# Low parts of weight blocks by a second rounding pass and an accumulating DMA instead of a GpSimd subtract

## The chip, the cores and the metric

The kernel runs on one core of one Trainium2 chip. Its time is device microseconds of one execution; times of a kernel are medians of several runs. A core has the engines TensorE (PE in the profile, PEld for its weight loads), VectorE (DVE), ScalarE (ACT), GpSimd (POOL) and SyncE (SP), which work side by side, each through its own instructions in order, and wait for each other through semaphores. DMAs are issued by an engine and done by 16 DMA engines.

## The reference

One step of a two-layer decoder trunk, 1024 wide, on 1056 tokens: one new sequence of 1024 and 8 sequences of 4 tokens each that go on from stored states. Layer 0 is an RG-LRU block, layer 1 an HGRN2 block with 8 heads of 128. What matters here is layer 1's input projection and what follows it in each head:

```
xn = _rmsnorm(x, g_norm)
u = (xn @ w_in).astype(float32)            # 1056 x 1024 times 1024 x 4096
q, f, iv, gate = split(u, 4, axis=-1)
q = silu(q)
log_g = logaddexp(log(lb), log1p(-lb) + log_sigmoid(f)); k = -expm1(log_g)
o, S_T = _hgrn2_chunked(q, k, iv, log_g, S0)
y = (rmsnorm over each head of o) * silu(gate)
x = x + y @ w_out
```

All of it is float32, and the outputs are the hidden states, the recurrent states and the normalised trunk output.

## The kernel before, in words

Tokens lie on the free axis, features on the 128 partitions. A float32 product is made of three matmuls in a faster format (`F32R`): each operand is split into a high part, which is the operand rounded to that format, and a low part, which is operand minus high part. `mm3` (lines 241 to 243) adds high times high, weight high times data low, and weight low times data high. In the profile the weight parts are named `whi` and `wlo`, and a raw weight block `wraw` (some raw blocks live in a piece of the tile `R`).

Layer 1 works head by head. For heads 0 and 1 the four projections are plain products of 352 columns. For heads 2 to 7 (`HC = 2`) two projections at a time are done by `seven`: the 256 outputs and the 1024 inputs and the 1056 tokens are halved, and seven products of half-size blocks take the place of eight. So there are twelve calls of `seven`, two for each head, the first for the projections 0 and 1 (q and f), the second for 3 and 2 (gate and v). One product is 24 matmuls of 264 columns. `FQ0`, `FQ` and `GV` give the order of the seven products (digits) and where in it the bursts of the heads' attention work (letters `b`) stand on TensorE.

A call of `seven` loads four raw blocks of 128 x 512 by SP (`dma`, line 308), forms the sums and differences that the scheme needs in place by `combine` on GpSimd (line 1431), and makes the high and low part of each of the seven blocks in `split`: ScalarE copies the raw block into the rounded format (line 1423), GpSimd subtracts that from the raw block (helper `subtract`, line 321 in the profile). High and low parts have rings of `NW = 4` buffers, so a split waits until the product four places earlier is done with its buffers. The raw blocks have five places, which go from one call to the next when their last split has read them. VectorE's `plus` (line 1504) and ScalarE's copies (line 1481) take the products out of PSUM; VectorE's operations of lines 1031 (decay scaling), 1053 and 1056 (masked copies) and 1519 belong to the attention and the activations of the heads.

The order of the work on every engine is set by a planner, the class `Flow`: each operation is added with an engine, an estimated time, what it reads and writes and a priority; `run` lists the operations by their latest starts and emits them in the order of the best plan found. There are two plans, one after the other: the first ends with layer 0 and the beginning of layer 1, the second holds all calls of `seven`. TensorE's main operations keep the order in which they are added. An operation with `both` set is a VectorE one that the plan holds back while GpSimd is busy. A DMA is an operation with a size `kb`, whose landing the plan estimates from it.

Of the kernel before, what the change touches and what calls it, by code (L numbers as in the profile page):

```python
# [14 lines left out]
F32 = mybir.dt.float32  # L15
# [3 lines left out]
AF = mybir.ActivationFunctionType  # L19
ALU = mybir.AluOpType  # L20
# [189 lines left out]
def tile_trunk(ctx: ExitStack, tc: tile.TileContext, xT, prm, hc, w0, wg, wo0, w1, wo1, s_in,  # L210
               yT, h_out, c_out, sp_out, ss_out):
    nc = tc.nc
    V, S, G, T, Q = nc.vector, nc.scalar, nc.gpsimd, nc.tensor, nc.sync
# [80 lines left out]
    with ExitStack() as l0:  # L294
        pl = l0.enter_context(tc.tile_pool(name="l0", bufs=1, reuse_waits="tile"))
        fl = Flow("PE")
# [9 lines left out]

        def dma(dst, src, r=(), w=(), prio=5, kb=180, q=Q):
            fl.add("SP" if q is Q else "ACT", 0.45, lambda: q.dma_start(dst, src), r, w, prio, kb * (1.0 if r else 0.75))

        def act(n, emit, r, w, prio=5, more=0.0):  # L310
            fl.add("ACT", 0.25 + 0.0007 * n + more, emit, r, w, prio)

        def dve(n, emit, r, w, prio=5, both=False):
            fl.add("DVE", 0.13 + 0.0011 * n, emit, r, w, prio, both=both)

        def pool(n, emit, r, w, prio=5):
            fl.add("POOL", 0.1 + 0.00245 * n, emit, r, w, prio)

        def subtract(e, n, b, x, a, r, w, prio):

            emit = lambda: e.tensor_tensor(b, x, a.bitcast(F32), op=ALU.subtract)  # L321
            if e is G:
                pool(n, emit, r, w, prio)
            else:
                dve(n, emit, r, w, prio, True)
# [38 lines left out]
        def weights(src, n, prio=2, e=G, at=None, q=Q, own=()):  # L364

            own = iter(own)
            got = []
            for a in range(0, n, 512):
                m = min(512, n - a)
                raw, *rk = next(own, None) or next(raws)  # L370
                if at:
                    (hi, hk), (lo, lk) = ((o[:, a:a + m], k) for o, k in at)
                else:
                    (hi, hk), (lo, lk) = next(his), next(los)
                dma(raw[:, :m], src[:, a:a + m], (), rk, prio, m / 2, q)
                act(m, lambda hi=hi, raw=raw, m=m: S.copy(hi[:, :m], raw[:, :m]), rk, (hk,), prio)  # L376
                subtract(e, m, lo[:, :m], raw[:, :m], hi[:, :m], (*rk, hk), (lk,), prio)
                got.append((hi, lo, hk, lk))

            def get(k):  # L380
                q = slice((k % 4) * 128, (k % 4 + 1) * 128)
                hi, lo, hk, lk = got[k // 4]
                return hi[:, q], lo[:, q], (hk, lk)

            return get
# [74 lines left out]
        def conv(g, head=False):  # L460

            items = []
            for j in range(3):
# [3 lines left out]
                def evac(c, ps, pk, by=None, j=j, m=m, mine=mine):  # L467
# [25 lines left out]
                    for src, dst, sh, u in parts:  # L493
                        act(u, lambda src=src, dst=dst, sh=sh: S.activation(dst, sh(src, 3), AF.Identity, bias=pc("cb", m),  # L494
                                                                         scale=pc("cw", 36 + m)), (xk, ("P",)), (tk,), 1, 0.1)
                        for k in range(3):
                            dve(u, lambda src=src, dst=dst, sh=sh, k=k: V.scalar_tensor_tensor(  # L497
                                dst, sh(src, k), pc("cw", 12 * k + m), dst, op0=ALU.mult, op1=ALU.add), (xk, tk), (tk,), 1, True)
                    w = slice(32 * j, 32 * j + 32)
                    dma(ST[w, chunk(c)], t[w], (tk,), (("ST", j, c),), 1, 45)  # L500
                    (a, ak), (b, bk) = xpart(j, 0, c), xpart(j, 1, c)
                    act(CH, lambda: S.copy(a, t), (tk,), (ak,), 1)
# [32 lines left out]
        def lru(g):  # L535
            for i, n in ((0, 4), (4, 2)):
                raw, rk = next(raws)
                u = 128 * n
                hi = gh[:, i:i + n, :].rearrange("p a b -> p (a b)")
                lo = gl[:, i:i + n, :].rearrange("p a b -> p (a b)")  # L540
                dma(raw[:, :u], wg[g][:, 128 * i:128 * i + u], (), (rk,), 2, u / 2)
                act(u, lambda raw=raw, hi=hi, u=u: S.copy(hi, raw[:, :u]), (rk,), (("gh", i),), 2)
                pool(u, lambda raw=raw, hi=hi, lo=lo, u=u: G.tensor_tensor(lo, raw[:, :u], hi.bitcast(F32), op=ALU.subtract),
                     (rk, ("gh", i)), (("gl", i),), 2)
# [297 lines left out]
        raw = (halves[1][:8], [slots[i] for i in (1, 4, 7, 2, 5, 8)] + [halves[1][8], free[8]], free[:8])  # L842
# [82 lines left out]
    with ExitStack() as l1:  # L925
        p1 = l1.enter_context(tc.tile_pool(name="l1", bufs=1, reuse_waits="tile"))
        fl = Flow(side=0.4)
# [468 lines left out]
        def seven(h, a, b, order, at=()):  # L1396
# [24 lines left out]
            def split(p):  # L1421
                (raw, rk), (hi, hk), (lo, lk) = slot[named[p]], next(his), next(los)
                act(512, lambda: S.copy(hi, raw), (rk,), (hk,), 2)  # L1423
                subtract(G, 512, lo, raw, hi, (rk, hk), (lk,), 2)
                parts[p] = hi, lo, (hk, lk)
                if p not in (1, 2):
                    freed.append(slot[named[p]])

            def combine(o, x, y, op):
                (o, ok), (x, xk), (y, yk) = slot[o], slot[x], slot[y]  # L1430
                pool(512, lambda: G.tensor_tensor(o, x, y, op=op), (xk, yk), (ok,), 2)

            split(1)
            split(2)
            combine("s", "21", "22", ALU.add)
            combine("21", "11", "21", ALU.subtract)
            combine("11", "s", "11", ALU.subtract)
            combine("12", "12", "11", ALU.subtract)
            for p in steps[2:NW]:
                split(p)  # L1440
# [15 lines left out]
            for c in order:  # L1456
# [8 lines left out]
                hi, lo, wk = parts[p]  # L1465
# [33 lines left out]
                n = steps.index(p) + NW  # L1499
# [70 lines left out]
        for k in range(H):  # L1570
            if k < 4:
                olds = [("x", 1, k, x) for x in range(2)] + [("T", 1, i, k, x) for i in range(2) for x in range(2)]
            else:
                n, i = ((2, 0), (3, 0), (4, 0), (4, 1))[k - 4]
# [66 lines left out]
        for m in range(KD):  # L1641
            row = (xh, xl)[m // 4][4 + m % 4]
            hi, lo, hk, lk = row[:, :nl], row[:, nl:2 * nl], ("late", m, 0), ("late", m, 1)
            for k in (hk, lk):
                inherit(k, [("x", p, m % 4, x) for p in (2, 3) for x in range(2)])
            raw, rk = next(raws)
# [60 lines left out]
        for a, n in OUT:  # L1707
# [4 lines left out]
            for m in range(KD):  # L1712
# [5 lines left out]
                hi, lo, wk = late[m]  # L1718
# [97 lines left out]
```

## Time and profile before

| what | us |
|---|---|
| runs, median of 3 | 1078.3 (1077.45 to 1078.73) |
| profiled execution, its own time | 1075.47 |
| its span, first to last instruction | 1073.7 |
| PE, PEld busy in the span | 1053.0, 1024.5 |
| DVE, ACT, POOL busy in the span | 808.2, 611.1, 558.0 |
| granted TensorE clock, mean | 0.996 |

The profile is of one execution. A group's row gives line, engine, operation, output from inputs, shape and count, then busy time and the mean of one in ns, then the engine's idle time before it and what ended that. A row of the timeline gives start, length, engine, line, operation and count, and in brackets the idle time before it. Matmul rows overlap, since matmuls are pipelined: a product's pace is read from the starts. A row of a stretch gives its limits, its length, busy time and count of PE, PEld, DVE, ACT and POOL, the granted clock, the share of the DMA engines and GB/s.

### The profile page before, as it was taken

The page shows a single profiled execution, that of the slowest core. Times are in us where ns is not written, and L with a number is a line of the kernel's source. Part 1 is how long each engine was busy: PE and PEld are TensorE (multiplying, and loading weights), DVE is VectorE, ACT ScalarE, POOL GpSimd, SP SyncE. Part 2 cuts the span into 40 slices and gives each one's busy share as a digit, 9 for nine tenths or more (in the row PEclk, how much of TensorE's full clock was granted, in tenths as well). Part 3 has the DMA queues.
Part 4 walks back from the last instruction along what each step waited for, and adds up shares of the span by engine and source line. Part 5 has one row for each costly group of instructions (what it writes and reads, how often), then busy time and mean ns, then how long its engine had stood idle before and what let it go on. Part 6 is the DMA issues. An engine that isn't in the chain of part 4 may idle for free.

```text
span 1073.7 us, 25345 instructions
## 1 busy us (share of the span) xinstructions
PE 1053.0 (98%) x9972; PEld 1024.5 (95%) x9972; DVE 808.2 (75%) x1535; ACT 611.1 (57%) x1395; POOL 558.0 (52%) x546
## 2 busy tenths in 40 slices
PE   9999999999999999999999998999999999999997
PEld 9999999999999999999998997999999999989996
DVE  8999996887997787283999997767768585774446
ACT  7578656867665964243364563747474655752323
POOL 3425353353543547455574854656566665541545
PEclk9999999999999999999999999999999999999998
DMA  9101112124832775240110121212121212354204
GB/s 302 59 27 43 56 49 71 58 61 126 271 104 66 222 252 176 103 131 34 60 51 24 49 92 43 100 43 91 35 92 41 91 44 80 116 169 160 85 1 162
DMA packets 70119, 103.05 MB, mean 96 GB/s; under 512 B 9200, under 2 KB 51184, under 8 KB 70000
## 3 DMA queue, kind: packets, MB, share of 16 engines
q1 hardware_dynamic: 67696, 98.67, 28.1%
q10 hardware_dynamic: 2304, 2.77, 0.8%
q8 instruction: 78, 1.28, 0.5%
q14 instruction: 41, 0.34, 0.1%
HBM read 71.05 MB, written 25.49 MB: 90 GB/s over the span
## 4 chain that ended last, share of the span: by engine, by line
PE 82%; DVE 14%; issue 1%; DMA 1%; ACT 1%; POOL 0%; SPq 0%; POOLq 0%; ACTq 0%; DVEq 0%
PE mm L241 23%; PE mm L242 22%; PE mm L243 22%; PE hg L1049 2%; DVE R L1363 1%; DVE R L1031 1%; PE hg L1266 1%; PE hg L565 1%; DVE tmp L1363 1%; PE hg L1158 1%; DVE a L1232 1%; PE hg L1268 1%; DVE sg L1031 1%; PE hg L241 1%; PE hg L242 1%
## 5 line engine op out<-in xcount | busy, mean ns | idle before, releaser
L241 PE MATMUL mm<-xh,whi 128*128 128x352 f32 (+1 forms) x1143 | 359.3, 314 | 7.2 <-DVE sg L1504 4.5
L242 PE MATMUL mm<-xl,whi 128*128 128x352 f32 (+1 forms) x1143 | 353.2, 309 | 0.0
L243 PE MATMUL mm<-xh,wlo 128*128 128x352 f32 (+1 forms) x1143 | 353.2, 309 | 0.0
L321 POOL TENSOR_TENSOR wlo<-wraw,whi 128x512 fp32r<-128x512 f32 (+2 forms) x131 | 175.9, 1351 | 168.7 <-ACT whi L376 83.6
L241 PEld LDWEIGHTS mm<-xh,whi 128*128 128x128 f32 x1143 | 214.7, 188 | 10.5 <-DVE sg L1504 6.0
L242 PEld LDWEIGHTS mm<-xl,whi 128*128 128x128 f32 x1143 | 215.0, 188 | 1.6 <-DVE xl L321 0.2
L243 PEld LDWEIGHTS mm<-xh,wlo 128*128 128x128 f32 x1143 | 214.9, 188 | 0.0
L497 DVE SCALAR_TENSOR_TENSOR k<-xb,prm_sb,k 128x352 f32<-128x352 f32 (+2 forms) x144 | 90.1, 637 | 10.9 <-ACT k L494 6.1
L241 PE MATMUL mm<-t,whi 128*128 128x264 f32 (+1 forms) x306 | 89.5, 293 | 0.0
L242 PE MATMUL mm<-t,whi 128*128 128x264 f32 (+1 forms) x306 | 87.7, 287 | 0.0
L243 PE MATMUL mm<-t,wlo 128*128 128x264 f32 (+1 forms) x306 | 87.5, 286 | 0.0
L580 POOL TENSOR_TENSOR k<-X 128x352 f32<-128x352 f32 x36 | 44.9, 1256 | 47.8 <-DVE R L581 38.6
L321 POOL TENSOR_TENSOR wlo<-R,whi 128x512 fp32r<-128x512 f32 x33 | 49.9, 1511 | 32.8 <-ACT whi L1423 28.9
L376 ACT CAST whi<-wraw 128x512 fp32r<-128x512 f32 (+2 forms) x83 | 46.0, 574 | 28.5 <-PE mm L242 16.9
L241 PEld LDWEIGHTS mm<-t,whi 128*128 128x128 f32 x306 | 57.6, 188 | 0.7 <-ACT k L1481 0.5
L1504 DVE TENSOR_TENSOR k<-mm,k 128x264 f32<-128x264 f32 x62 | 26.5, 430 | 41.5 <-PE mm L243 41.4
L243 PEld LDWEIGHTS mm<-t,wlo 128*128 128x128 f32 x306 | 57.7, 188 | 0.0
L242 PEld LDWEIGHTS mm<-t,whi 128*128 128x128 f32 x306 | 57.6, 188 | 0.0
L1031 DVE TENSOR_TENSOR R<-R,sg 128x512 f32<-128x512 f32 (+1 forms) x48 | 50.4, 1050 | 0.1
L241 PE MATMUL mm<-yh,whi 128*128 128x352 f32 x153 | 49.9, 326 | 0.0
L243 PE MATMUL mm<-yh,wlo 128*128 128x352 f32 x153 | 49.4, 323 | 0.0
L242 PE MATMUL mm<-yl,whi 128*128 128x352 f32 x153 | 49.4, 323 | 0.0
(415 smaller groups left out, 2684.6 us busy)
## 6 DMA issues: line engine op xcount, KB each, us to landing
wraw<-in_w_dram SPq DMA_DIRECT2D x91, 256.0 KB, 2.6
wraw<-in_wo_dram SPq DMA_DIRECT2D x34, 192.0 KB, 2.5
si<-in_s_in_dram SPq DMA_DIRECT2D x8, 512.0 KB, 4.2
out_ss_out_dram<-si SPq DMA_DIRECT2D x8, 512.0 KB, 2.6
sg<-x1b SPq DMA_DIRECT2D x21, 176.0 KB, 2.8
x<-sg SPq DMA_DIRECT2D x21, 176.0 KB, 1.8
R<-in_w_dram SPq DMA_DIRECT2D x14, 256.0 KB, 2.5
R<-td SPq DMA_DIRECT2D x72, 44.0 KB, 2.0
```

The costliest lines, as they stand in the source:

```text
L241: T.matmul(out, wh, xh, start=first, stop=False, skip_group_check=chained)
L242: T.matmul(out, wh, xl, start=False, stop=False, skip_group_check=chained)
L243: T.matmul(out, wl, xh, start=False, stop=last, skip_group_check=chained)
L321: emit = lambda: e.tensor_tensor(b, x, a.bitcast(F32), op=ALU.subtract)
L376: act(m, lambda hi=hi, raw=raw, m=m: S.copy(hi[:, :m], raw[:, :m]), rk, (hk,), prio)
L497: dve(u, lambda src=src, dst=dst, sh=sh, k=k: V.scalar_tensor_tensor(dst, sh(src, k), pc("cw", 12 * k + m), dst, op0=ALU.mult, op1=ALU.add ...
L565: fl.add("PE", 0.62, lambda ps=ps, i=i, c=c: T.matmul(ps[:96, :CH], gs[:, i, :], ST[:96, chunk(c)], start=True, stop=True), (("gs",), *((" ...
L580: pool(CH, lambda x=x, a=a, b=b: G.tensor_tensor(x, a.bitcast(F32), b.bitcast(F32), op=ALU.add), (ak, bk), (xk,), 3)
L1031: dve(n // 2, lambda sv=sv, dv=dv, s=s, f=f: V.tensor_tensor(dv[:, :, s, :], sv[:, :, s, :], f, op=ALU.mult), (*sk, *gk), dk if i == o els ...
L1049: T.matmul(ps[32 * j:32 * j + 32, n * w:n * w + w], B[:, o:o + 32], q(slice(o, o + 32)), start=True, stop=True, tile_position=(0, 32 * j))
L1363: dve(n, lambda: V.tensor_tensor(o, a, b, op=op), r, (w,), prio, True)
L1504: dve(QT, lambda: V.tensor_tensor(o[0], z[0], u[0], op=ALU.add), (z[1], u[1]), (o[1],), 0)
```

## The change

`split` makes the low part in another way. ScalarE makes the high part as before. The low part's buffer is first filled by a second ScalarE pass, which writes the negated raw block rounded to the same format; then a DMA issued by GpSimd's queue adds the raw block to it where it lies, in float32. The sum is raw block minus rounded raw block, the same low part. The low part no longer reads the high part, and the raw block is read by the DMA until this has landed. GpSimd no longer subtracts in `split`. Other users of `subtract` stay as they are. For the planner the DMA is an operation of 0.93 on GpSimd with a landing.

```diff
         def dma(dst, src, r=(), w=(), prio=5, kb=180, q=Q):
             fl.add("SP" if q is Q else "ACT", 0.45, lambda: q.dma_start(dst, src), r, w, prio, kb * (1.0 if r else 0.75))
+
+        def low(n, dst, src, r, w, prio=5):
+
+            act(n, lambda: S.activation(dst, src, AF.Copy, scale=-1.0), r, w, prio)
+            fl.add("POOL", 0.93, lambda: G.dma_start(dst.bitcast(F32), src, accum_op=ALU.add), (*r, *w), w, prio, n / 2)
...
                 act(512, lambda: S.copy(hi, raw), (rk,), (hk,), 2)
-                subtract(G, 512, lo, raw, hi, (rk, hk), (lk,), 2)
+                low(512, lo, raw, (rk,), (lk,), 2)
                 parts[p] = hi, lo, (hk, lk)
```

## The prediction

> **What bounds the kernel now.** I read the page first, for the engine that is full.
>
> ```profile
> span 1073.7 us, 25345 instructions
> PE 1053.0 (98%) x9972; PEld 1024.5 (95%) x9972; DVE 808.2 (75%) x1535; ACT 611.1 (57%) x1395; POOL 558.0 (52%) x546
> ```
>
> PE (TensorE matmul) is busy 98% of the span, and the change takes nothing from it. It can only touch gaps of PE, so the next view is a table of stretches. The seven products of heads 2 to 7 run from about 589 to 926 us; what lies before 589 belongs to a first plan that the diff leaves as it is. Columns: PE, PEld, DVE, ACT, POOL busy.
>
> ```profile
> 589.00:667.00 78.00, 74.08 (x942) 70.21 (x944) 68.22 (x117) 42.57 (x123) 49.36 (x38) 1.00 0.18 64
> 725.00:783.00 58.00, 57.23 (x859) 55.15 (x846) 40.58 (x82) 34.11 (x91) 36.10 (x29) 1.00 0.19 67
> 926.00:1074.00 148.00, 138.43 (x1254) 132.67 (x1242) 81.12 (x184) 55.40 (x153) 63.83 (x68) 0.97 0.36 118
> ```
>
> The first head loses 78.00 - 74.08 = 3.9 us of PE, an ordinary head 0.77. The view of waits, cut to 589:926 and PE, says what ended these gaps:
>
> ```profile
> PE mm L241 <- DVE sg L1504: 4.3, 6, 0.8
> PE mm L241 <- DVE attns L1056: 2.7, 1, 2.7
> ```
>
> That is all: 7.0 us, and each time PE waits for DVE. No gap of this stretch is ended by the low parts themselves. So 7.0 us is the most that the change can win here, and the question is why DVE is late. The timeline of the longest gap shows it (start, length, engine):
>
> ```profile
> 642.15 4.46 DVE L1519 SCALAR_TENSOR_TENSOR sg<-sg,k 128x264 f32<-128x264 f32 x1
> 641.56 1.04 POOL L1190 TENSOR_TENSOR vb<-vst,bm 96x512 fp32r<-96x512 f32 x1 [1.58 <-DVE vst L1174]
> 642.56 1.27 POOL L321 TENSOR_TENSOR wlo<-wraw,whi 128x512 fp32r<-128x512 f32 x1
> 643.79 1.30 POOL L321 TENSOR_TENSOR wlo<-R,whi 128x512 fp32r<-128x512 f32 x1
> 645.05 1.27 POOL L1431 TENSOR_TENSOR wraw<-R,wraw 128x512 f32<-128x512 f32 x1
> 646.40 1.36 POOL L1431 TENSOR_TENSOR R<-R,wraw 128x512 f32<-128x512 f32 x1
> 650.24 0.39 PE L241 MATMUL mm<-xh,whi 128*128 128x264 f32 x1 [2.70 <-DVE attns L1056]
> ```
>
> A DVE operation with two operands in SBUF took 4.46 us while POOL went through a mask, two of the subtracts that the change removes (L321) and two block sums without a pause. The small waits have the same cause:
>
> ```profile
> 763.02 1.28 POOL L1431 TENSOR_TENSOR wraw<-R,wraw 128x512 f32<-128x512 f32 x1
> 763.16 1.69 DVE L1031 TENSOR_TENSOR sg<-sg 128x512 f32<-128x512 f32 x1
> 767.90 0.68 DVE L1031 TENSOR_TENSOR R<-R,sg 128x512 f32<-128x512 f32 x1
> 768.99 0.39 PE L241 MATMUL mm<-xh,whi 128*128 128x264 f32 x1 [0.77 <-DVE sg L1504]
> ```
>
> The same operation takes 0.68 us free and 1.69 us when a POOL sum got in first. DVE then runs without a gap up to the evacuation for which PE waits 0.77 us. The 1.0 us lost at 763 is more than that wait.
>
> **The change, part by part.** Twelve calls of `seven` with seven splits each make 84. Rows for 589:926 (83 subtracts are recorded):
>
> ```profile
> L321 POOL TENSOR_TENSOR wlo<-wraw,whi 128x512 fp32r<-128x512 f32 x50 | 67.0, 1344 | 63.8 <-ACT whi L1423 53.1 <-PE mm L243 6.8 <-PE hg L1049 3.9
> L321 POOL TENSOR_TENSOR wlo<-R,whi 128x512 fp32r<-128x512 f32 x33 | 49.9, 1511 | 32.8 <-ACT whi L1423 28.9 <-PE hg L1049 3.9
> L1423 ACT CAST whi<-wraw 128x512 fp32r<-128x512 f32 x51 | 31.4, 619 | 25.1 <-PE mm L242 13.5 <-issue 11.3
> L1423 ACT CAST whi<-R 128x512 fp32r<-128x512 f32 x33 | 20.5, 622 | 16.6 <-PE mm L242 8.3 <-issue 7.5 <-POOL wlo L321 0.7
> wraw<-in_w_dram SPq DMA_DIRECT2D x91, 256.0 KB, 2.6
> si<-in_s_in_dram SPq DMA_DIRECT2D x8, 512.0 KB, 4.2
> 719.69 0.33 SPq L308 DMA_DIRECT2D wraw<-in_w_dram  x1
> ```
>
> Removed: 67.0 + 49.9 = 117 us of POOL. Added on ACT: 84 x 0.62 = 52 us, one more pass like the cast of the high part; ACT in an ordinary head goes from 34.1 to 34.1 + 14 x 0.62 = 42.8 of 58 us, so it still has gaps. Added on POOL: 84 issues. No POOL issue is in this trace; the bounds are an SP issue, 0.33, and a subtract, 1.51. I take 0.95, the middle (the planner books 0.93). Landing is unknown too: the accumulation reads 256 KB twice and writes 256 KB. A plain load of 256 KB lands 2.6 us after issue, one of 512 KB 4.2; these are the nearest rows, and I take 3.4 between them, with 8.4 (twice the larger) as far end, and nothing below 2.6, as it moves more. A low part then comes 0.62 + 0.95 + 3.4 = 5.0 us after its buffer is free, not 1.4 after the high part.
>
> **Does PE wait for that?** In the ordinary head the shortest way from a freed buffer to its use is that of product 6 of the second `seven`:
>
> ```profile
> 740.28 0.28 PE L241 MATMUL mm<-xh,whi 128*128 128x264 f32 x1
> 741.54 0.60 ACT L1423 CAST whi<-wraw 128x512 fp32r<-128x512 f32 x1
> 749.32 0.28 PE L243 MATMUL mm<-t,wlo 128*128 128x264 f32 x1
> ```
>
> The buffer is free at 740.28 and the low part is needed at 749.32: 9.04 us. ACT's delay of 1.26, the pass 0.62, the issue 0.95 and two hops of 0.1 leave 6.0 us for the landing. At 3.4 the cost is nothing; the cover is these two and a half products on PE, and it is gone at 6.0. The block sums that overwrite a raw block now wait for the landing of the DMA that reads it; POOL stands meanwhile with the next sums, vb masks and square roots behind it, but that chain ends at the same buffer, which frees last. SP's loads into the freed raw blocks, in order on their queue, also wait for the landing, 5.0 - 1.4 = 3.6 us longer than for the subtract; what they feed is the same chain of sums.
>
> The first `seven` has less lead:
>
> ```profile
> 589.36 0.62 ACT L1423 CAST whi<-wraw 128x512 fp32r<-128x512 f32 x1
> 590.06 1.29 POOL L321 TENSOR_TENSOR wlo<-wraw,whi 128x512 fp32r<-128x512 f32 x1 [2.25 <-ACT whi L1423]
> 593.10 1.49 POOL L1431 TENSOR_TENSOR wraw<-R,wraw 128x512 f32<-128x512 f32 x1
> 594.43 0.29 PE L243 MATMUL mm<-xh,wlo 128*128 128x264 f32 x1
> 600.31 0.28 PE L243 MATMUL mm<-t,wlo 128*128 128x264 f32 x1
> ```
>
> If the low pass goes ahead of the high one, the issue runs from 590.06 to 591.0 and lands at 594.4, just in time for 594.43. The block sum that overwrites this raw block moves from 593.10 to 594.4 and ends at 595.9; a pass, an issue and two hops, 1.77, bring 597.7, the landing 601.1, against 600.31: 0.8 us lost once. At 2.6 nothing is lost, at 4.2 it is 0.8 + 1.6 = 2.4.
>
> **The gain.** Without the two subtracts the 4.46 us operation finds a pause in POOL after the mask, so I count the 2.7 us as won. Of the 4.3 us I count half, 2.1: the sums that held DVE remain, only moved behind a landing. Sum: -2.7 - 2.1 + 0.8 = -4.0 us. The profiled execution took 1075.47 us (span 1073.7 and 1.8 around it), so it would take 1071.5; it lies 2.8 below the median of the runs, 1078.3, from which I forecast 1074.3. All 7.0 us won would be 1071.3, half the forecast's gain 1076.3: the forecast's own range.
>
> The Trainium skill (SBUF — State Buffer, section "SBUF: two separate sides") says that a VectorE operation with two SBUF inputs and a GpSimd operation that reads SBUF lock each other out for a whole instruction; the 4.46 us row agrees. It also speaks against this change: GpSimd cannot write the descriptors of its own DMA while VectorE is in a two-port mode, which no run here shows yet. That is the last rival below.
>
> **Rivals.** (1) *No relief*: the sums hold DVE wherever they go, and the start costs 0.8: 1079.1. For it: at 763 the holder was a sum, not a subtract. (2) *The landing is late*, the mechanism on the other side. It decides from 6.0 us. At 8.4, each of six heads loses 2.4 us at product 6, 14.4; at the start the first low part is 5.0 late (599.4 against 594.43) and product 6 another 5.7: 25 us, 1103. For it: three passes over 256 KB, next to 512 KB state transfers. Against it: no row of a transfer of this size is above 4.2. (3) *ACT is late*:
>
> ```profile
> 729.12 0.38 ACT L1481 COPY k<-mm 128x264 f32<-128x264 f32 x1
> 730.31 0.29 PE L241 MATMUL mm<-t,whi 128*128 128x264 f32 x1
> ```
>
> PE reuses this bank 0.8 us after its copy ends. One pass of 0.62 in front fits, both passes (1.24) cost 0.44 us; at two places in each of the twelve calls that is 10.6 at most, half of it 5.3, with the start 6.1: 1084.4. (4) *The issue is held by DVE* as the subtract was (shortest 1.27, here up to 1.51 on the mean): no relief, and everything behind the issue 0.8 later, as with a landing of 4.2, so the start costs 2.4: 1080.7.
>
> **How the numbers follow.** Forecast 0.42; (1) 0.18; (4) 0.07; (3) 0.15; (2) 0.18. About 0.2%, 2.2 us, is what a measurement here can tell from no change. Faster is the forecast, 0.42; within it (1), 0.18; slower the other three, 0.40. The range 1071 to 1087 leaves out most of (2) and holds the other cases, 0.82.
>
> **What would show it.** In the profile after: the 2.70 us wait before the matmul at 650 gone, the long L1519 near 1 us; POOL's stretch in an ordinary head near 36.1 - 14 x 0.45 = 29.8, ACT's near 42.8; DVE's below 40.6; PE's gap per head under 0.77. I am wrong if PE waits for a DMA on wlo in every head (2), for ACT L1481 (3), or if DVE's L1031 means stay as they are (1).

## The result, and the profile after

The changed kernel took 1075.75 us (median of 20 runs, 1073.60 to 1080.73), the kernel before 1077.91 (20 runs, 1076.32 to 1079.82). The ratio is 0.9982, with an interval of 0.9973 to 0.9992: faster by 0.2%, some 2 us. The forecast was a gain of 4.0 us, to a median of 1074.3. The profiled execution went from 1075.47 to 1073.76 us, by -1.7, so the two profiles stand to each other about as the medians do.

The page's first lines of the changed kernel:

```profile
span 1071.9 us, 25510 instructions
PE 1053.5 (98%) x9972; PEld 1026.6 (96%) x9972; DVE 758.7 (71%) x1535; ACT 651.5 (61%) x1479; POOL 513.9 (48%) x546
```

ScalarE has 84 operations more (1395 to 1479) and 40 us more. GpSimd has as many as before (an issue for each subtract) and 44 us less. The line to dwell on is DVE: the same 1535 instructions, 49.5 us less (808.2 before). None of them was changed; they are held less.

Stretches as before (columns PE, PEld, DVE, ACT, POOL busy, granted clock, DMA share, GB/s):

```profile
589.00:667.00 78.00, 75.90 (x1062) 72.81 (x1062) 54.56 (x124) 54.01 (x146) 38.23 (x40) 1.00 0.59 128
725.00:783.00 58.00, 58.00 (x817) 56.12 (x816) 33.77 (x84) 41.55 (x106) 29.18 (x30) 1.00 0.60 131
926.00:1074.00 148.00, 135.61 (x1191) 130.36 (x1189) 77.52 (x181) 52.76 (x149) 61.70 (x66) 0.95 0.36 116
```

The ordinary head has no gap of PE left (0.77 before); DVE went from 40.6 to 33.8, POOL from 36.1 to 29.2, ACT from 34.1 to 41.6. The first head still loses 2.1 us. The last stretch has 12.4 us without PE where it had 9.6, but 2.1 us of it now lie behind the end of the span (0.3 before), so it needs a finer division, which follows below.

Two of the operations of DVE that the prediction followed, from the table of groups for 589 to 926, first before, then after (name, shape, count, busy time, mean ns):

```profile
L1519 DVE SCALAR_TENSOR_TENSOR sg<-sg,k 128x264 f32<-128x264 f32 x22 | 16.7, 765 | 0.6 <-ACT sg L1518 0.3
L1031 DVE TENSOR_TENSOR sg<-sg 128x512 f32<-128x512 f32 x11 | 14.2, 1291 | 0.0
```

```profile
L1524 DVE SCALAR_TENSOR_TENSOR sg<-sg,k 128x264 f32<-128x264 f32 x22 | 9.0, 428 | 4.5 <-ACT sg L1523 4.5
L1036 DVE TENSOR_TENSOR sg<-sg 128x512 f32<-128x512 f32 x11 | 8.9, 805 | 21.0 <-PE hg L1054 21.0
```

Line numbers are 5 higher after. The operation that had taken 4.46 us once is gone to a mean of 428 ns over all 22, and none of the four of its form in that first head is above 435 ns.

PE's waits, 520 us to the end, in the changed kernel; then those of the kernel before that lie outside 589 to 926 (us in total, times, longest):

```profile
PE mm L241 <- ACT xh L1595: 3.4, 1, 3.4
PE hg L1054 <- DVE sg L1036: 2.3, 1, 2.3
PE mm L241 <- DVE sg L1509: 1.5, 2, 1.1
PE hg L1108 <- DVE a L1036: 1.1, 1, 1.1
PE mm L243 <- DMA wlo<-wraw: 1.0, 1, 1.0
```

```profile
PE hg L1049 <- DVE R L1061: 2.0, 1, 2.0
PE mm L241 <- ACT xh L1590: 1.4, 1, 1.4
PE mm L242 <- DVE xl L321: 0.8, 1, 0.8
```

Of the 7.0 us of waits in the seven products, 1.5 for DVE are left and 1.0 for a landing is new. But the waits outside are different ones: 2.3 + 1.1 at 541 us for 2.0 at 565, and 3.4 ahead of the tail (the trunk's last products) for 1.4 + 0.8.

To see what that makes, I divided each profiled span at the first and at the last matmul of 264 columns of line 241, the first and last product of the sevens:

| stretch | before | after | difference |
|---|---|---|---|
| up to the first product of the sevens | 594.19 | 595.67 | +1.5 |
| first to last product | 350.18 | 344.46 | -5.7 |
| from there to the end | 129.33 | 131.77 | +2.4 |
| span | 1073.7 | 1071.9 | -1.8 |

The stretch that the prediction reckoned with won more than it had said. Two thirds of that were lost in stretches that it had left out.

How the new operation does, from the view of its line (ns: shortest, median, longest) and the table of DMA issues (us from issue to landing):

```profile
L313 POOL DMA_DIRECT2D wlo<-wraw x51: 843/867/1185, 591.8 to 922.8; - x51
L313 POOL DMA_DIRECT2D wlo<-R x33: 852/877/1192, 593.1 to 919.5; - x33
DMA to landing us min/median/max: 3.3/4.2/6.8
```

The issue costs 0.87 us (taken: 0.95). The landing of 4.2 us is counted from the start of the issue and so holds the issue: a block sum that waits for the DMA issued from 591.81 to 592.88 starts at 595.46, only 2.6 us behind the issue's end, less than the shortest landing in the view. The prediction added the two, 0.95 + 3.4 = 4.35 us, and its limit of 6.0 behind the issue is 6.95 when counted from its start.

### The profile page after: what moved, and what is told of

It reads as the page before. It is cut to its first block, busy times and chain, and to the rows that moved or that the text cites. A ratio compares the mean times of both kernels' runs of the same rounds, so it can differ in the third digit from the quotient of the medians.

```text
span 1071.9 us, 25510 instructions
## 1 busy us (share of the span) xinstructions
PE 1053.5 (98%) x9972; PEld 1026.6 (96%) x9972; DVE 758.7 (71%) x1535; ACT 651.5 (61%) x1479; POOL 513.9 (48%) x546
## 4 chain that ended last, share of the span: by engine, by line
PE 89%; DVE 7%; DMA 1%; issue 1%; ACT 1%; POOL 0%; POOLq 0%; ACTq 0%; SPq 0%; DVEq 0%
PE mm L241 24%; PE mm L242 24%; PE mm L243 24%; PE hg L1054 2%; PE hg L1163 2%; PE hg L1271 1%; PE hg L570 1%; PE hg L1217 1%; PE hg L1273 1%; PE hg L241 1%; PE hg L242 1%; PE hg L243 1%; DVE R L1368 1%; DVE R L1036 1%; PE hg L1315 1%
## 5 line engine op out<-in xcount | busy, mean ns | idle before, releaser
L326 POOL TENSOR_TENSOR wlo<-wraw,whi 128x512 fp32r<-128x512 f32 (+1 forms) x80 | 108.2, 1363 | 101.7 <-ACT whi L381 92.3
L313 POOL DMA_DIRECT2D wlo<-wraw x51 | 44.9, 883 | 51.9 <-ACT wlo L312 38.1
L313 POOL DMA_DIRECT2D wlo<-R x33 | 30.1, 913 | 49.5 <-ACT wlo L312 49.1
```

Of the source, the lines that this page charges most:

```text
L313: fl.add("POOL", 0.93, lambda: G.dma_start(dst.bitcast(F32), src, accum_op=ALU.add), (*r, *w), w, prio, n / 2)
```

## The experiments

The theory: GpSimd's operations that read SBUF hold DVE's two-operand operations; taking the subtracts away frees DVE, and the planner, which is given the new operations, orders the work for them. Rivals: that the new order alone does it; that the new work alone does it, whatever the order; that the place of the subtracts decides; and, for what was lost, that the price of the landing in the plan is too low, or that PE's clock falls behind gaps.

### Order and work apart

**The order of after with the work of before.** The plan is given both ScalarE passes and the DMA's prices, but one pass and the subtract are executed:

```diff
-                act(512, lambda: S.copy(hi, raw), (rk,), (hk,), 2)
-                low(512, lo, raw, (rk,), (lk,), 2)
+                todo = [lambda: S.copy(hi, raw)]
+                once = lambda: todo.pop()() if todo else None
+                act(512, once, (rk,), (hk,), 2)
+                act(512, once, (rk,), (lk,), 2)
+                fl.add("POOL", 0.93, lambda: G.tensor_tensor(lo, raw, hi.bitcast(F32), op=ALU.subtract), (rk, lk), (lk,), 2, 256)
```

> The instruction order of the changed kernel, but the low parts made as before: one ScalarE pass and GpSimd's subtract in the place of the DMA. Theory A (GpSimd's two-input subtracts held VectorE, and their going is the gain; the new order only costs, 1.5 us ahead of the seven products and 2 us behind them): the waits of TensorE for VectorE in the seven products come back, 5 to 7 us, and with the order's 3.5 us the time is 2 to 5 us above before, ratio 1.002 to 1.005. Theory B (the gain is the other order that the planner found): the sevens stay 5 us shorter, ratio about 0.998 as the changed kernel, and VectorE's busy time falls below 780 us.

Measured: 1084.91 us, ratio 1.0071 (1.0058 to 1.0084), above the 1.002 to 1.005 expected. DVE is back at 811.2 us. PE's waits, the first at the start, the others from 589 to 950:

```profile
PE hg L1054 <- DVE sg L1036: 2.4, 1, 2.4
...
PE mm L241 <- DVE k L1512: 3.0, 1, 3.0
PE mm L241 <- DVE sg L1512: 2.3, 5, 0.7
PE mm L241 <- ACT k L1489: 1.7, 5, 0.8
```

The second row is five short waits for the same evacuation, one in nearly every head, as before the change. The order doesn't free DVE. It also has, in the first row, the start's wait of 2.4 us that the changed kernel has and the kernel before has not, and none of the new operations: that wait comes from the order.

**The work of after in the order of before.** Both passes stand where the one stood and the DMA where the subtract stood. The plan keeps the prices of what they replace, so the order is that of before:

```diff
-                act(512, lambda: S.copy(hi, raw), (rk,), (hk,), 2)
-                subtract(G, 512, lo, raw, hi, (rk, hk), (lk,), 2)
+                def passes():
+                    S.activation(lo, raw, AF.Copy, scale=-1.0)
+                    S.copy(hi, raw)
+
+                act(512, passes, (rk,), (hk,), 2)
+                pool(512, lambda: G.dma_start(lo.bitcast(F32), raw, accum_op=ALU.add), (rk, hk), (lk,), 2)
```

> The instruction order of before, with the low parts made as in the change: both ScalarE passes stand where the one stood, low part first, and the DMA stands where the subtract stood. Theory A: the first plan, the start and the tail are as before (first product of the sevens at 594.2, the tail as long as before), the sevens win 4 to 6 us, less up to 2 us where the order did not allow for a landing of 4.2 us: 1072 to 1074.5, ratio 0.994 to 0.9965. Theory B: nothing won, ratio 1.000 or above, since the order is that of before and the landings are late.

Measured: 1084.22 us, ratio 1.0063 (1.0043 to 1.0083), although DVE has 753.1 us, as little as after. By the theory a gain had been expected, to 1072 to 1074.5 us. Waits of all engines in four heads (684 to 912):

```profile
ACT wlo L1424 <- POOL wraw L1435: 27.2, 7, 5.3
POOL wraw L1435 <- DMA wlo<-wraw: 26.7, 8, 4.9
POOL R L1435 <- DMA wlo<-R: 18.6, 6, 5.9
DVE sg L1040 <- ACT ST L1517: 18.7, 4, 5.3
```

Read from below: DVE waits for ScalarE, which stands in order behind a low pass, which waits for a block sum, which waits for the DMA that still reads the block. The changed kernel has the same view with 17.6 and 7.8 us for the two waits on landings, and none of ScalarE for a block sum: its plan knows the landing and puts other work there. So neither half of the change gains; the gain is of both together. Freeing DVE by 50 us is worth nothing where ScalarE is queued behind landings.

### What holds DVE

To the changed kernel, after each accumulating DMA of heads 3 to 7 (70 of them), an operation is added on GpSimd that the plan doesn't know and whose result nobody reads: in the first kernel a subtract with two operands in SBUF, in the second a memset of the same tile.

```diff
+                    if h > HC:
+                        G.tensor_tensor(idle_, raw, raw, op=ALU.subtract)
```

```diff
+                    if h > HC:
+                        G.memset(idle_, 0.0)
```

> The changed kernel, and in heads 3 to 7 a GpSimd subtract of the same size behind each accumulating DMA, of which the planner knows nothing; it reads the raw block twice and writes an unused tile. Theory A: VectorE's busy time rises by 30 to 40 us, towards 790 to 800, and in these heads TensorE waits for VectorE again, 0.5 us or more a head: 2.5 to 6 us above the changed kernel, ratio to before 1.000 to 1.004. Theory B: GpSimd has the room (28 of 58 us in a head), ratio 0.998 and VectorE's busy time stays near 759.

> As the run with the added subtract, but the added GpSimd operation is a memset of the same unused tile, which reads nothing. Theory A with the hold tied to operations that read SBUF: VectorE's busy time stays within 10 us of 759 and the ratio within 0.001 of the changed kernel's 0.998. If any busy GpSimd holds VectorE: VectorE's busy time rises in proportion to the memset's length as in the run with the subtract.

Measured: 1092.37 us, 1.0138 (1.0122 to 1.0154) with the subtract; 1075.61 us, 0.9986 (0.9977 to 0.9994) with the memset, as the changed kernel. A line of the page with the subtract and one with the memset:

```profile
PE 1060.9 (97%) x9972; PEld 1032.4 (95%) x9972; DVE 816.2 (75%) x1535; ACT 649.7 (60%) x1479; POOL 583.4 (53%) x616
```

```profile
PE 1056.1 (98%) x9972; PEld 1029.6 (96%) x9972; DVE 758.9 (71%) x1535; ACT 651.9 (61%) x1479; POOL 552.5 (51%) x616
```

Both add 70 instructions to GpSimd. The memset raises GpSimd's busy time by 38.6 us and DVE's by 0.2; the subtract raises GpSimd's by 69.5 and DVE's by 57.5, more than the 30 to 40 expected, and costs 17 us of the kernel. So what holds DVE isn't that GpSimd is busy: the subtract reads SBUF, the memset doesn't. The rule of the Trainium skill quoted in the prediction (SBUF — State Buffer, "SBUF: two separate sides") agrees with both runs.

With the subtract PE waits, from 589 to 950, also behind ScalarE, which stands in order for a DVE result (18.2 us for line 1036 from 684 to 926, 7.8 in the changed kernel) with its copies behind it:

```profile
PE mm L241 <- ACT k L1494: 8.0, 5, 2.6
PE mm L241 <- DVE sg L1517: 3.6, 3, 1.3
```

The group of DVE shows the hold in the mean of one form, 805 ns in the changed kernel; here with the subtract, then with the memset (whose 1008 is a shift within DVE, since all of DVE together gained 0.2 us):

```profile
L1036 DVE TENSOR_TENSOR sg<-sg 128x512 f32<-128x512 f32 x11 | 24.5, 2227 | 18.5 <-PE hg L1054 18.5
```

```profile
L1036 DVE TENSOR_TENSOR sg<-sg 128x512 f32<-128x512 f32 x11 | 11.1, 1008 | 21.0 <-PE hg L1054 21.0
```

### Does the place of the subtracts decide?

The DMA only in the first of a head's two calls of `seven`, then only in the second; the other call keeps the subtract. The plan knows what each does.

```diff
+                if a:
+                    subtract(G, 512, lo, raw, hi, (rk, hk), (lk,), 2)
+                else:
+                    low(512, lo, raw, (rk,), (lk,), 2)
```

> Low parts by the DMA only in the first call of each head (q and f, 42 blocks), the subtract in the second. Theory A puts the gain where the long holds were: the subtracts of the next first call stood straight ahead of two block sums (642 to 647 and 760 to 766 of before), in front of product 3 of the second call, where all seven waits for VectorE ended. So this half brings most of the relief: sevens 3 to 5 us shorter, VectorE's busy time near 785, ratio 0.996 to 0.999 with the start and the tail as the plan makes them.

> Low parts by the DMA only in the second call of each head (gate and v). The subtracts ahead of product 3 of the second call stay, so by theory A the waits there stay: sevens at most 2 us shorter, VectorE's busy time near 785, ratio 0.999 to 1.003. If it is the sum of GpSimd's time that counts and not the place, this half gains as much as the other.

Measured: 1078.46 us, 1.0004 (0.9992 to 1.0017) with the DMA in the first call, 1076.15 us, 0.9986 (0.9975 to 0.9997) with the DMA in the second, whose interval takes in the whole change's ratio. DVE has 792.2 and 771.4 us, both between before and after. PE's waits with the first call only, 589 to 950:

```profile
PE mm L241 <- DVE sg L1512: 4.1, 5, 1.3
```

These are the small waits of before (4.3, 6 times) at nearly their full length. I had expected the first call to bring most of the gain, since its subtracts lie beside the attention's long DVE operations; that fell. The second call frees more of DVE (36.8 us against 16.0).

The profiles show where the gain of each half is. From the first to the last product of the sevens the first call alone takes 349.2 us and the second alone 348.6, where it was 350.2 before and is 344.5 with both. The halves do not add up to the whole (1.0 + 1.6 against 5.7). With the first call only, the wait of 2.7 us is gone, but a wait of 1.7 us for an evacuation and one of 1.0 us for a landing are new. With the second only, the long wait stays (2.6 us), and the small ones shrink from 4.3 to 1.3. Outside the sevens the first half loses 3.3 us and the second 2.1. So 16 us less of DVE shortens the sevens by 1.0 us, and in this profile the stretches around them take that back.

### The prices in the plan

The plan books the landing 3.6 us behind the start of the issue (2.6 + 256/250), where 4.2 were measured. Booked 1.0 us later, at 4.6:

```diff
-            fl.add("POOL", 0.93, lambda: G.dma_start(dst.bitcast(F32), src, accum_op=ALU.add), (*r, *w), w, prio, n / 2)
+            fl.add("POOL", 0.93, lambda: G.dma_start(dst.bitcast(F32), src, accum_op=ALU.add), (*r, *w), w, prio, n)
```

and, in a second kernel, the plan also doesn't let the issue of a DMA hold DVE:

```diff
-            if both and free["POOL"] > t0:
-                us = max(us, free["POOL"] - t0 + us - 0.13)
+            if both and held > t0:
+                us = max(us, held - t0 + us - 0.13)
...
+            if e == "POOL" and not kb:
+                held = end
```

> The changed kernel, but the plan books a landing 1.0 us later (the DMA's size in the plan is 512 instead of 256), nearer to the 4.2 us that the trace of the changed kernel shows. If the plan's knowledge of the landing decides whether the change pays, TensorE's wait for wlo in the first seven (1.0 us) goes and the sums stand less long before a landing; the time is 1 to 2 us below the changed kernel, ratio to before 0.996 to 0.998. If the plan's order is as good as chance, the time is within 3 us of the changed kernel on either side, for a gap in another place.

> As the run with the later landing, and the plan no longer holds VectorE's two-input operations back while GpSimd issues a DMA. The run with the memset showed that only reading operations of GpSimd hold VectorE, so the plan is nearer to the chip: 1 to 3 us below the changed kernel, ratio 0.995 to 0.998. If order is chance: within 3 us of it on either side.

Measured: 1075.23 us, 0.9971 (0.9961 to 0.9981) with the landing priced; 1082.52 us, 1.0036 (1.0024 to 1.0048) with both. The interval of the first overlaps that of the changed kernel, so no gain of it is shown. Nor did PE's waits for low parts go, as expected; from 589 to 950 they grew from 1.0 us:

```profile
PE mm L243 <- DMA wlo<-wraw: 2.7, 2, 2.3
```

The second kernel lost 7 us against the first, against the expectation. Its longest waits of PE, 520 to the end:

```profile
PE mm L245 <- DMA wlo<-wraw: 5.0, 2, 3.9
```

That low parts come later because DVE's work is planned earlier is a guess. The wait isn't all of the loss either: in the profiles 3.4 us of it lie ahead of the first product of the sevens and 4.3 between the first and the last.

### The tail, and PE's clock

The changed kernel's stretch around the wait of 3.4 us ahead of the tail, in slices of 2 us (PE, PEld, DVE, ACT, POOL, then the granted clock):

```profile
940.00:942.00 2.00, 0.65 (x6) 0.44 (x4) 2.00 (x4) 0.72 (x3) 0.97 (x2) 1.00 0.81 253
942.00:944.00 2.00, 0.00 (x0) 0.00 (x0) 1.58 (x7) 1.28 (x4) 0.00 (x0) 1.00 0.76 219
944.00:946.00 2.00, 1.91 (x6) 1.61 (x7) 2.00 (x5) 0.41 (x1) 0.00 (x0) 0.56 0.92 281
946.00:948.00 2.00, 2.00 (x10) 2.00 (x9) 0.52 (x2) 0.91 (x2) 0.52 (x1) 0.58 0.93 316
```

PE stands for 3.4 us and then works for about 4 us at 0.57 of its clock: 1.91 x 0.44 + 2.00 x 0.42 = 1.7 us more. With a wait that is 3.4 - 1.4 - 0.8 = 1.2 longer (1.35 and 0.77 unrounded make it 1.25), that is 2.9 against the +2.4 measured; the 0.5 between them is not assigned.

To test the clock's part, 16 spare matmuls of 128x128 on a tile of ones, whose result is overwritten, stand ahead of the tail's first product. They add work that the reference doesn't have.

```diff
+        def spares(o, k, n):
+            for _ in range(n):
+                fl.add("PE", 0.0, lambda: T.matmul(o, ones, ones, start=True, stop=True), (), (k,), 1, main=True)
...
-            ps, pk = product(ws2[m], yparts(c), 8 if m > 1 else 1)
+            ps, pk = product(ws2[m], yparts(c), 8 if m > 1 else 1, spare=0 if n else 16)
```

> The changed kernel with 16 spare matmuls (128x128, 0.153 us each by the warm-up row, 2.45 us) ahead of the first product of the tail, where TensorE waits 3.4 us for ScalarE's split of a reloaded block; the plan books them at nothing. Clock theory (the wait in the tail also costs the granted clock, 0.56 for the 4 us behind it, some 1.7 us): the wait falls below 1 us, the granted clock behind it is 1.00, and the time from the first to the last instruction behind the sevens is 1.5 to 2 us shorter; ratio to before 0.996 to 0.997. If the clock's fall is not tied to the wait, or the spare matmuls only delay the product: 0.998 or above.

> The run with the landing priced at its measured length, with 14 spare matmuls ahead of the tail's first product and 9 and 2 ahead of the two diagonal products of head 0 (gaps of 1.7 and 0.5 us near 541 us, behind which other runs showed a granted clock of 0.5 for some 6 us). Clock theory: the fall of the clock behind the tail's wait (0.5 to 0.72 for 8 us in that run's profile, some 3.5 us) goes, ratio 0.9935 to 0.996, and the times of single executions spread less than the 7 us of the changed kernel. Against it: 0.997 as without the spare matmuls.

> The kernel before with 8 spare matmuls (1.2 us) ahead of the tail's first product, where TensorE waits 1.35 us. In its profile no fall of the clock is seen there (1.00), so by the clock theory hardly anything is won: ratio 0.999 to 1.001. If spare matmuls win as much here as in the changed kernel, they do something else than hold the clock.

Measured: 1074.17 us, 0.9966 (0.9953 to 0.9978) for the changed kernel with 16 spares. 1074.90 us, 0.9967 (0.9956 to 0.9979) for the kernel with the landing priced, 14 spares in the tail and 11 in the first head at the start. 1077.92 us, 0.9999 (0.9990 to 1.0008) for the kernel before with 8 spares. The first, in order of time and in slices:

```profile
940.75 3.73 PE L394 MATMUL mm<-ones 128*128 128x128 f32 x32
944.23 0.41 PE L241 MATMUL mm<-xh,t 128*128 128x352 f32 x1
```

```profile
944.00:946.00 2.00, 2.00 (x15) 1.86 (x14) 2.00 (x6) 0.34 (x1) 0.00 (x0) 1.00 0.91 274
946.00:948.00 2.00, 2.00 (x14) 2.00 (x13) 1.00 (x3) 0.00 (x0) 0.00 (x0) 1.00 0.95 293
```

The tail starts when it did (944.23 against 944.01): its input sets that, and the spares only fill the wait. But the clock behind it stays at 1.00, and the tail, from the last product of the sevens, shrinks from 131.77 to 129.5 us. Of these 2.25 us, 1.7 come ahead of the last row of small products (line 275), as worked out above. The other 0.6 comes behind it, where the clock had fallen to 0.50 in the changed kernel and was still at 1.00 here, so that the tail is as short as before (129.33) is in part chance.

One profile could be chance as a whole, since the clock doesn't fall behind every such wait. The others speak for the wait, too. In nine profiles of this study PE waits 2.4 to 3.7 us ahead of the tail without spares, and in eight of them the clock behind it falls below 0.7 (not in that of the order of after with the work of before, wait 2.6). In the two with 16 and 14 spares it stays at 1.00, and with 14 the tail is 130.35 us for 132.49 without. For the medians, 0.9966 against 0.9982 is near the size that it should be (1.7 us), with intervals that overlap.

The two other kernels gained nothing by spares that can be told from the kernels that they were added to (0.9967 against 0.9971, 0.9999 against 1). In the kernel before, the wait ahead of the tail is short, and there was little to win.

## Why the prediction was right, and where it was not

**The mechanism and its sign were right.** Each wait was put down to DVE, and DVE to GpSimd's operations that read SBUF; the added subtract and the added memset show that. What the prediction named as its signs came: the wait of 2.70 us gone, the long operation at 0.43 (said: near 1), POOL's ordinary head at 29.2 (said 29.8), ACT's at 41.6 (42.8), DVE's 33.8 (below 40.6), PE's gap per head 0 (under 0.77).

**The costs of the added work were near.** The issue took 0.87 us for 0.95. The passes took 53.0 us by their own rows for 52 (84 of 0.63), while ScalarE's busy time as a whole rose by 40. Issue and landing together took 4.2 us for 4.35. That this fits is in part luck: the rows for plain loads, from which 3.4 was taken, are counted from the start of the issue, and the prediction added an issue once more. With the measured 4.2 its sum for the start of the first call gives 0.5 us of loss in place of 0.8, by the old order; the chip, in the new order, showed one wait on a low part of 0.99. No wait in an ordinary head ended on a landing, as forecast: the limit was 6.95 from the start of the issue, the longest landing 6.8.

**The gain in the sevens was mis-sized, to the low side.** I counted half of the 4.3 us of small waits, since the block sums stay and hold DVE wherever they go. All but 1.5 us went. What is left shows that the reason was sound, though. DVE and POOL of the changed kernel, in order of time:

```profile
649.08 2.55 DVE L1036 TENSOR_TENSOR R<-R,sg 128x512 f32<-128x512 f32 x1
```

```profile
647.40 1.28 POOL L1436 TENSOR_TENSOR wraw<-R,wraw 128x512 f32<-128x512 f32 x1 [1.38 <-DMA wlo<-wraw]
648.63 0.20 POOL L1095 COPY ab<-R 128x32 f32<-128x32 f32 x1
648.80 1.03 POOL L1195 TENSOR_TENSOR vb<-vst,bm 96x512 fp32r<-96x512 f32 x1
649.80 1.28 POOL L1436 TENSOR_TENSOR R<-R,wraw 128x512 f32<-128x512 f32 x1
```

A mask and a block sum without a pause stretch a DVE operation to 2.55 us, and the evacuation that ends PE's one larger wait (1.10 us, before the matmul at 652.02) starts right behind it, at 651.55. It is the old mechanism with two holders where there were four. (The prediction counted a fifth, the second block sum. That is recorded from 646.40, and the operation, some 0.4 us long when free, ended at 646.61, so it had got in ahead of it.) By waits the sevens gained 7.0 - 1.5 - 1.0 = 4.5 us; the table of stretches has 5.7. The other 1.2 us is in PE's busy time: 342.9 us from the first to the last product before and 341.7 after, with 4832 matmuls recorded between them in both. Where they follow each other closer is open.

**The step that failed** is the claim that "what lies before 589 belongs to a first plan that the diff leaves as it is", together with the fact that nothing was counted behind 926. The planner's second plan takes in heads 0 and 1 as well as the tail, and it is made anew as a whole when the operations of the sevens change: on VectorE the two kernels go through the same order up to about 515 us and differ from there. Before 589 this put 2.34 + 1.08 us of waits at 541 in place of 2.0 at 565: +1.4 of the +1.5. The order without the new work has waits of 2.4 and 1.1 us there too, and the new work in the old order has the 2.0 us at 565, so it is the order and not the work. Behind 926 it put a longer wait, and the slow clock behind that: +2.4. Without these 3.9 us the profiled execution would have been 5.7 faster, more than the 4.0 forecast; with them it was 1.8 of span. So the forecast came as near as it did because two misses cancel in part: 1.7 us too little in the sevens and 3.9 us left out around them.

**The rivals.** No relief is excluded by DVE's 49 us. The landing that decides is excluded in the order of after (one wait of 0.99 on a low part), but it is what happens in the order of before: there landings hold block sums, those hold ScalarE, and the kernel is 0.6% slower. So that rival was real, and the plan is what kept it out. ScalarE late was not seen in the sevens of the changed kernel: no wait on line 1486 is in its view. The issue held by DVE was not seen: 1.19 us is the longest of 84. What makes some landings as long as 6.8 us stays open.

**What stays open:** why PE's wait for ScalarE ahead of the tail is longer in all five orders made for the DMA (2.4 to 3.4 us, 1.4 before); why a price nearer to the chip loses 7 us; and where the 1.2 us of the sevens beside the waits come from.

## What to carry to other kernels

Where GpSimd does elementwise work on SBUF beside a loaded VectorE, count what it costs VectorE and not only what it costs GpSimd: here 70 subtracts cost GpSimd 69.5 us and VectorE another 57.5, and 70 memsets cost VectorE 0.2. When an order is made by a planner, a change in one stage can re-order every stage of the same plan; find out first how far that plan reaches, and keep a sum for each stage, since the part outside the change can take back most of the gain. And a change that trades short operations for a longer latency has to be tried together with an order that knows the latency: each half alone was slower here than the kernel before.

## What was not expected of the hardware

**Gaps of 2 to 3.4 us may or may not be followed by a slow clock.** In the first profile of the kernel before, the wait of 2.70 us at 650 is followed by a clock of 1.00, as is the one of 2.0 at 565. In the profile of the same kernel with spare matmuls in the tail, which has the same two waits, of 2.0 and 2.7, both are followed by a low clock (granted clock: third column from the end):

```profile
568.00:572.00 4.00, 3.79 (x76) 3.62 (x77) 3.94 (x5) 1.50 (x4) 4.00 (x4) 0.57 0.23 72
652.00:654.00 2.00, 1.64 (x12) 1.64 (x12) 1.86 (x8) 0.63 (x1) 0.00 (x0) 0.91 0.00 0
654.00:656.00 2.00, 1.91 (x9) 1.60 (x9) 1.93 (x6) 0.62 (x1) 1.09 (x1) 0.50 0.00 0
```

The same holds for the changed kernel's order near 541 us. Behind its waits of 2.3 and 1.1 us the clock stayed at 1.00 in its profile and fell in that of the kernel with 16 spares in the tail, whose order up to there is the same. The two rows:

```profile
544.00:546.00 2.00, 2.00 (x69) 1.97 (x54) 1.96 (x4) 1.03 (x2) 1.25 (x1) 1.00 0.00 0
544.00:546.00 2.00, 2.00 (x57) 1.97 (x42) 1.96 (x4) 1.03 (x2) 1.25 (x1) 0.60 0.00 0
```

The first product of the sevens came at 595.67 us in the one and at 597.30 in the other. So stretches of two single profiles can differ by 1.6 us from this alone, and the start's +1.5 is sound only because the waits themselves differ and the clock there is 1.00 in both profiles compared.

The Trainium skill (TensorE: Matmul & The Clock Gate, "Part 1: The HAM clock gate") has a free-running window of about 3.4 us that must be idle before the clock falls. That the phase differs from run to run agrees with these pairs; that it takes a whole idle window does not, since the clock fell behind waits of 2.0 and 2.7.

The mean granted clock recorded with each run points the same way: 0.9948 over the 58 runs of the kernel before that were taken beside the experiments, 0.9933 over the 20 after, 0.9952 over the 5 with spares in the tail. 0.0015 of 1072 us is 1.6 us, as an estimate, which is of the size of what the tail's clock lost. Within the 20 runs after, 0.001 of clock goes with 0.8 us of time (correlation -0.68), so it is also a part of their spread of 7 us.

**A matmul of fp32 operands is recorded twice:** the 16 spare ones, on a tile not in the faster format, stand as x32 in the row shown above, 3.73 us for all, 0.23 for each of the 16.

**An accumulating DMA of 256 KB within SBUF** lands 4.2 us after its issue starts at the median, as a plain load of 512 KB did before (4.2), with the traffic of a head doubled (67 to 131 GB/s) and no wait of PE on it in an ordinary head.
